# A two-layer diffusion-transformer step on one core: modulation by row sums, w_in's upper parts by casting loads, staged parameters

## The chip, the cores and the metric

The kernel runs on one core of one Trainium2 chip. The metric is the device time of one execution in microseconds. The core has five engines that run their own instruction queues in order: TensorE (PE, with its weight loads as PEld), VectorE (DVE), ScalarE (ACT), GpSimd (POOL) and SyncE (SP). Transfers between HBM and the on-chip memory are issued from the queues of SP, ACT or POOL.

## The reference

Two layers run over 256 latent tokens and 128 context tokens of width 1024, in float32. Each layer computes a modulation, a mixer of 16 heads and a SwiGLU feed-forward part:

```
m   = silu(c) @ w_mod + b_mod              (c: one vector for the latent tokens, one for the context; 6 x 1024 columns)
h   = rms(x) * g_mix * (1 + m[1]) + m[0]
z   = h @ w_in                             (1024 x 2336: q/kv latents, neighbourhood q,k,v, differential q,k,v)
x  += m[2] * (concat(o_mla, o_na, o_df) @ w_out)
h   = rms(x) * g_ffn * (1 + m[4]) + m[3]
x  += m[5] * ((silu(h @ w_gate) * (h @ w_up)) @ w_down)        (inner width 2816)
```

The three mixers are multi-head latent attention (6 heads), two-dimensional neighbourhood attention with learned biases (6 heads) and differential attention (4 heads). The new keys and values of the context are outputs too.

## The kernel before, in words

Tokens lie on the free axis of x (128 partitions x 8 x 384). A product with a weight is made of three float32r matmuls (`mm3`, lines 317 to 320): the weight and the activations are split into an upper part, rounded to float32r, and the rest. For weights, `split_hi` (line 251) copies the raw float32 block to `wh` on ACT, and `split_lo` (line 257) subtracts it on DVE into `wl`. There are three buffers each of raw, `wh` and `wl`; a `wh` buffer is free again when PE has read it for the last time.

**Modulation.** `ModSet` (lines 334 to 403) makes 2048 columns of m: for each of 8 row blocks of 128, one 1 MB load on SP's queue into a raw buffer and four matmuls that have the two vectors as 32 stationary columns (line 369), in four column groups of the array side by side. The set is then copied out on ACT (line 375), turned by four transposes (line 380) and added to b_mod on DVE (line 386). The first 2048 columns of layer 0 are made in four parts before its first norm. The other sets are spread over the stages as follows: layer 0's attention has both remaining sets of layer 0 and the first of layer 1 (24 blocks); the turn from layer 0 to layer 1 has 6 blocks of layer 1's second set, four of which lie in `early` buffers that POOL's queue loads (lines 1549 to 1553); layer 1's attention has the last 2 of these and the third set (10 blocks).

**Attention.** The order of all instructions of a layer's attention is written out by a planner (`Plan.order`, lines 112 to 176): a list scheduler with a duration for each task, one queue per engine, counted buffers (`ROOM`) and priorities. Each engine then gets its tasks in the planned order. `g1` (line 750) multiplies by w_in in 6 column chunks of 4 row blocks each; its tasks and the modulation blocks have low priorities, so the planner puts them between the steps of the softmax chains. `weights` (line 725) plans the load of a block, the upper part on ACT and the lower part on DVE. POOL makes the inverse roots of the norms in this stage (`rsqrt`, lines 509 and 510), which queries and keys wait for, and two-operand steps of the differential heads.

**Feed-forward part.** It is not planned by hand: the framework's scheduler orders the instructions by priority and estimated time. `w_get` makes the parts of a weight block two blocks ahead. A gate/up step m (22 of them) has 48 matmuls, a down step (8 of them) has 66. The buffers `hh` and `hl`, which hold the mixer's input and later its outputs, are free in this stage; `fh` and `fl` hold the input of the gate/up loop.

**Parameters.** `parameters(l)` (line 530) fetches a row of per-column gains to all partitions (`prow`, line 534) and makes rotary tables from it on DVE. For layer 1 the fetch is issued from POOL's queue and is placed as soon as layer 0 has read `prow` for the last time.

## Time and profile before

| what | value |
|---|---|
| median of 3 runs | 1043.28 us (1042.18 to 1043.92) |
| the profiled execution's own time | 1044.4 us |
| its span | 1042.2 us |
| mean granted TensorE clock | 0.995 |
| PE / DVE / ACT / POOL busy | 98% / 61% / 49% / 14% of the span |
| moved by DMA | 160.14 MB, of it 4.69 MB by POOL's queue |

The profile is of one execution. Busy times leave out register, branch, semaphore and DMA-issuing instructions. In the lists of groups a row gives the line, the engine, the operation, what it writes and reads with the shapes, the count, then the busy time in us and the mean of one in ns, then the idle time before them and what ended it. A float32 matmul leaves two records, so a modulation block of four shows as x8.

### The profile page before, as it was taken

Reading aid. Unit: us, or ns where it says so; the run is one execution under the profiler, and the core shown is the slowest. Engines: PE = TensorE matmul, PEld = TensorE weight load, DVE = VectorE, ACT = ScalarE, POOL = GpSimd, SP = SyncE. Lnnn points to the kernel's source line nnn. Section 1 sums busy time; section 2 is a strip of 40 time slices with the busy share of each in tenths; the row PEclk is TensorE's granted clock in tenths of the full one; section 3 lists DMA queues with packets and bytes.
Section 4 is the critical chain, followed back from the end, with each engine's and each line's share of the span. In section 5 each row is a group of like instructions: output and inputs, shape, how many; then the busy total and the mean of one; then the engine's idle time right before and its main releaser. Section 6 shows DMA issues by size and latency. Waiting matters only on the chain.

```text
span 1042.2 us, 16578 instructions
## 1 busy us (share of the span) xinstructions
PE 1025.5 (98%) x6212; PEld 931.2 (89%) x6212; DVE 630.9 (61%) x1447; ACT 509.0 (49%) x1179; POOL 149.9 (14%) x221
## 2 busy tenths in 40 slices
PE   8999999999999999999999999999999999999998
PEld 7877777669999999999978977777999999999998
DVE  4677786767555555544446887777756555554332
ACT  3376777745433443333326567786644333343221
POOL 2266223200000000000016543240000000000000
PEclk9999999999999999999999999999999999999999
DMA  9865548745625343364444245552334344333541
GB/s 360 317 206 185 165 152 298 256 136 161 203 82 161 93 151 111 96 207 123 128 159 155 73 150 169 189 185 81 122 109 135 110 133 122 120 111 111 148 133 45
DMA packets 125999, 160.14 MB, mean 154 GB/s; under 512 B 4704, under 2 KB 111328, under 8 KB 120800
## 3 DMA queue, kind: packets, MB, share of 16 engines
q1 hardware_dynamic: 123552, 153.73, 45.9%
q0 software_dynamic: 784, 4.69, 1.2%
q8 instruction: 49, 0.80, 0.3%
q10 hardware_dynamic: 1584, 0.66, 0.2%
q14 instruction: 30, 0.25, 0.1%
HBM read 156.02 MB, written 3.05 MB: 153 GB/s over the span
## 4 chain that ended last, share of the span: by engine, by line
PE 88%; POOL 4%; DVE 4%; ACT 2%; issue 1%; DMA 1%; ACTq 0%; DVEq 0%; POOLq 0%
PE z L318 13%; PE z L320 12%; PE z L319 12%; PE t L319 6%; PE t L318 6%; PE t L320 6%; PE s L319 6%; PE s L318 6%; PE s L320 6%; PE m L369 4%; PE s L996 3%; POOL small L510 3%; PE t L963 2%; PE t L1098 2%; PE t L1335 1%
## 5 line engine op out<-in xcount | busy, mean ns | idle before, releaser
L251 ACT ACTIVATE wh<-raw 128x1024 fp32r<-128x1024 f32 (+2 forms) x216 | 201.6, 935 | 356.0 <-PE z L319 128.9
L257 DVE TENSOR_TENSOR wl<-raw,wh 128x1024 fp32r<-128x1024 f32 (+2 forms) x216 | 231.2, 1072 | 122.8 <-ACT wh L251 122.6
L318 PE MATMUL z<-fh,wh 128*128 128x386 f32 x304 | 103.2, 339 | 0.0
L319 PE MATMUL z<-fl,wh 128*128 128x386 f32 x304 | 103.0, 339 | 0.0
L320 PE MATMUL z<-fh,wl 128*128 128x386 f32 x304 | 102.6, 338 | 0.0
L318 PE MATMUL z<-wh,hh 128*128 128x384 f32 (+1 forms) x264 | 100.5, 381 | 0.9 <-ACT tok L1203 0.4
L320 PE MATMUL z<-wh,hl 128*128 128x384 f32 (+1 forms) x264 | 90.4, 342 | 0.5 <-DVE hl L490 0.3
L319 PE MATMUL z<-wl,hh 128*128 128x384 f32 (+1 forms) x264 | 89.7, 340 | 0.0
L510 POOL TENSOR_TENSOR small<-small,mhalf 128x4 f32<-128x4 f32 (+4 forms) x58 | 72.2, 1245 | 4.8
L318 PE MATMUL s<-fh,wh 128*128 128x386 f32 x200 | 68.2, 341 | 0.0
L318 PE MATMUL t<-fh,wh 128*128 128x386 f32 x200 | 68.1, 340 | 0.0
L319 PE MATMUL s<-fl,wh 128*128 128x386 f32 x200 | 67.8, 339 | 0.0
L319 PE MATMUL t<-fl,wh 128*128 128x386 f32 x200 | 67.7, 339 | 0.0
L320 PE MATMUL t<-fh,wl 128*128 128x386 f32 x200 | 67.5, 338 | 0.0
L320 PE MATMUL s<-fh,wl 128*128 128x386 f32 x200 | 67.5, 338 | 0.0
L1015 ACT ACTIVATE e<-s,small 128x384 f32<-128x384 f32 (+1 forms) x108 | 54.3, 509 | 16.3 <-DVE small L1004 15.2
L318 PEld LDWEIGHTS z<-wh,hh 128*128 128x128 f32 x264 | 49.8, 189 | 13.1 <-issue 8.2
L319 PEld LDWEIGHTS z<-fl,wh 128*128 128x128 f32 x304 | 57.5, 189 | 0.0
L320 PEld LDWEIGHTS z<-fh,wl 128*128 128x128 f32 x304 | 57.3, 188 | 0.0
L318 PEld LDWEIGHTS z<-fh,wh 128*128 128x128 f32 x304 | 57.2, 188 | 0.0
L996 PE MATMUL s<-ku,qu 96*128 96x384 f32 (+5 forms) x170 | 52.0, 411 | 0.6 <-ACT e L1015 0.6
L319 PE MATMUL z<-ul,wh 128*128 128x384 f32 x154 | 52.4, 340 | 0.0
(305 smaller groups left out, 2321.1 us busy)
## 6 DMA issues: line engine op xcount, KB each, us to landing
raw<-in_w_mod SPq DMA_DIRECT2D x36, 1024.0 KB, 5.1
raw<-in_w_gate SPq DMA_DIRECT2D x22, 1024.0 KB, 5.4
raw<-in_w_up SPq DMA_DIRECT2D x22, 1024.0 KB, 5.4
raw<-in_w_down SPq DMA_DIRECT2D x32, 704.0 KB, 4.5
raw<-in_w_in SPq DMA_DIRECT2D x40, 384.0 KB, 4.0
raw<-in_w_out SPq DMA_DIRECT2D x8, 1024.0 KB, 5.9
qu<-in_w_mod SPq DMA_DIRECT2D x8, 512.0 KB, 6.7
ku<-in_w_mod SPq DMA_DIRECT2D x8, 512.0 KB, 7.4
```

The source lines that it names most:

```text
L251: nc.scalar.activation(hi, src, AF.Copy)
L257: nc.vector.tensor_tensor(lo, src, hi.bitcast(F32), op=ALU.subtract)
L318: nc.tensor.matmul(out, sh, mh, start=first, stop=False)
L319: nc.tensor.matmul(out, sh, ml, start=False, stop=False)
L320: nc.tensor.matmul(out, sl, mh, start=False, stop=last)
L369: nc.tensor.matmul(self.pm[32 * g:32 * g + 32, :n], sv[:, kb + k, :], ws, start=(kb + k == 0), stop=(kb + k == KD - 1), tile_position=(0, ...
L510: nc.gpsimd.tensor_tensor(out, t[:, :n], mhalf[:, :n], op=ALU.pow)
L963: nc.tensor.transpose(pt[:, b, :], x, ident)
L996: nc.tensor.matmul(ps[:, i, :], q, k, start=True, stop=True)
L1015: nc.scalar.activation(x["e"][i], ps[:, j, :], AF.Exp, bias=x["mx"][:, i:i + 1], accum_out=x["su"][:, i:i + 1])
L1098: nc.tensor.matmul(po[64 * i:64 * i + 64, 0:NL], vv[:, b, v0 + i, :], p["pT"][i][:, b, :], start=(b == 0), stop=(b == 2), tile_position=(0 ...
L1335: nc.tensor.matmul(po, x["p"][:, b, :], vd[0][:, b if t < 2 else 3, h, :], start=(b == 0), stop=(b == nb - 1))
```

## The change

**Modulation.** 40 of the 96 column blocks of 128 are no longer made by matmuls: columns 5120 to 6143 of both layers, and columns 0 to 2047 and 4096 to 5119 of layer 1. A new class `RowSums` makes them on DVE in the feed-forward stages. It loads 128 rows of the transposed w_mod (0.5 MB, POOL's queue, three buffers in the room of `hl`), multiplies them by silu(c), which lies in the room of `hh` on all partitions, and adds up along the row with one `tensor_tensor_reduce` for each of the two vectors, starting from b_mod. Layer 0's stage makes one block after each of the gate/up steps 2 to 21 and then 2, 3, 3 and 4 after the first four down steps; layer 1's stage makes one after each of the gate/up steps 2 to 9. The remaining sets are columns 2048 to 4095 of each layer (8 blocks) and columns 4096 to 5119 of layer 0 (4 blocks, each two row blocks of 1024 columns). The `early` loads follow the last row sum, in the room of `fh`, `fl`, `hh` and `hl`.

**w_in.** From chunk 2 on in layer 0 and from chunk 1 on in layer 1 (16 and 20 blocks) the upper part is not copied by ACT: a load from HBM on POOL's queue writes float32r into the `wh` buffer. The raw block is loaded as before, and DVE subtracts as before. The planner has a POOL task of 0.55 for the issue, in the line of the blocks, that takes the `wh` buffer, and a transfer task after it.

**Parameters.** Layer 1's row is loaded into the room of `fl0` and copied to `prow` by ACT.

The host adds the transposed w_mod and the two vectors in rows to the inputs. `RowSums.load` issues as many loads as there are buffers; each further one waits until DVE has read the buffer.

```diff
@@ -38,7 +38,11 @@
 PARAM = (28, 11)
 LAG = 2.8
 SPREAD = ((15, 3), (60, 9))
-DOWN = (0, 0, 0, 0, 0, 0, 0, 0)
+ROWSUMS = ((0, (40, 48)), (1, (0, 16)), (1, (32, 40))), ((1, (40, 48)),)
+ROWS_UP = (0, 0) + (1,) * 20
+ROWS_DOWN = (2, 3, 3, 4, 0, 0, 0, 0)
 PPRIO = (1.0, 2.0, 3.0, 4.0)
 WPRIO = (1.5, 2.5, 3.5, 4.5)
@@ -52,7 +56,8 @@
 PDN, PDD, PDU, PRT1, PRX, PRN, PRM, PRS = (-1.0, -2.0, -6.0, 0.6, 0.0, 0.0, 0.0, 1.0)
 NORMP = -1100.0
 HOPS = {('pe', 'act'): 0.2, ('pe', 'dve'): 0.16, ('act', 'pe'): 0.22, ('dve', 'pe'): 0.27, ('pool', 'dve'): 0.06, ('act', 'dve'): 0.15, ('dve', 'act'): 0.15}
-EXTRA = (8, 135, 7)
+CAST = (2, 1)
 ROOM = {'z': 3, 's': 2, 't': 2, 'raw': 3, 'graw': 2, 'w': 3, 'tok': 4, 'brief': 2, 'row': 5, 'un': 3, 'e': 4, 'pT': 3, 'pd': 2, 'bias': 2}
 CHUNKS = (((0, 416),),) + tuple(tuple((c + 128 * p, 128) for c in (1568, 1824, 2080)) for p in range(2)) + tuple(
...
@@ -334,30 +339,30 @@
     class ModSet:
-        def __init__(self, l, q, pre=(), part=None):
-            self.l, self.q, self.pre, self.w = l, q, pre, {}
+        def __init__(self, l, n, runs, part=None, pre=()):
+            self.l, self.n, self.part, self.pre, self.w = l, n, part, pre, {}
+            self.runs, self.per = runs, 4 // len(runs)
+            self.cols = [c + n * i for c in runs for i in range(self.per)]
+            self.step = 512 // n
             self.kb = 0
-            if part is None:
-                self.n, self.cols = 512, [2048 * q + 512 * g for g in range(4)]
+        def load(self, kb, *kind):
+            if kb < len(self.pre):
+                self.w[kb] = [self.pre[kb].rearrange("p (k c) -> p k c", k=1)]
+                return
+            nr, width = len(self.runs), self.n * self.per
+            if kind and kind[0] == "un":
+                t = [v.rearrange("p h t -> p (h t)")[:, :1024].rearrange("p (k c) -> p k c", k=self.step) for v in self.room()]
             else:
-                n = self.n = 512 // PARTS
-                self.cols = [2 * n * part, 2 * n * part + n, 1024 + 2 * n * part, 1024 + 2 * n * part + n]
-            self.part, self.step = part, 512 // self.n
-        def load(self, kb, *kind):
-            if self.part is not None and kind[0] != "raw":
-                t = [v.rearrange("p h t -> p (h t)")[:, :1024] for v in self.room()]
-            elif self.part is not None:
-                t = raw.tile([P, 2, 1024], F32, tag="raw", name=nm("raw"))
-                t = [t[:, i] for i in range(2)]
-            if self.part is not None:
-                for i in range(2):
-                    nc.sync.dma_start(t[i], w_mod0[self.part, kb // self.step, :, i])
-                self.w[kb] = [v.rearrange("p (k c) -> p k c", k=self.step) for v in t]
-            elif kb < len(self.pre):
-                self.w[kb] = self.pre[kb]
-            elif self.part is None:
-                self.w[kb] = load(mod_rows(self.l, kb, self.cols[0]), [2048])
+                t = raw.tile([P, nr, self.step, width], F32, tag="raw", name=nm("raw"))
+                t = [t[:, i] for i in range(nr)]
+            for i, c in enumerate(self.runs):
+                src = w_mod[self.l, kb * P:(kb + self.step) * P, c:c + width].rearrange("(k p) c -> p k c", p=P)
+                if self.part is not None:
+                    src = w_mod0[self.part, kb // self.step, :, i].rearrange("p (k c) -> p k c", k=self.step)
+                nc.sync.dma_start(t[i], src)
+            self.w[kb] = t
         def mm(self, kb):
@@ -365,8 +370,8 @@
                 for g in range(4):
-                    ws = w[:, g * n:(g + 1) * n] if self.part is None else w[g // 2][:, k, (g % 2) * n:(g % 2) * n + n]
-                    nc.tensor.matmul(self.pm[32 * g:32 * g + 32, :n], sv[:, kb + k, :], ws,
+                    i = g % self.per
+                    nc.tensor.matmul(self.pm[32 * g:32 * g + 32, :n], sv[:, kb + k, :], w[g // self.per][:, k, i * n:(i + 1) * n],
                                      start=(kb + k == 0), stop=(kb + k == KD - 1), tile_position=(0, 32 * g))
@@ -388,11 +393,11 @@
                 mod_aff(self.l, 0, KD // PARTS * self.part, KD // PARTS * (self.part + 1))
-            elif self.q != 1:
-                mod_aff(self.l, self.q // 2, 0, KD)
+            elif self.cols[0] == 4 * DM:
+                mod_aff(self.l, 1, 0, KD)
         def steps(self):
-            for kb in range(self.kb, KD):
+            for kb in range(self.kb, KD, self.step):
                 self.load(kb)
@@ -416,6 +421,35 @@
             pcol[l][:, g0 + k0:g0 + k1].unsqueeze(2).to_broadcast([P, k1 - k0, 2]), op0=ALU.add, op1=ALU.mult)
+    class RowSums:
+        def __init__(self, parts):
+            self.todo = [(l, c) for l, (a, b) in parts for c in range(a, b)]
+            room = act.tile([P, 3 * DM], F32, tag="hh", name=nm("sums"))
+            self.s, self.junk = room[:, :2 * DM].rearrange("p (v k) -> p v k", v=2), room[:, 2 * DM:]
+            self.w = act.tile([P, 3, DM], F32, tag="hl", name=nm("wt"))
+            self.n = self.loaded = 0
+            nc.gpsimd.dma_start(self.s, crow_d.unsqueeze(0).to_broadcast([P, 2, DM]))
+            self.load()
+            nc.scalar.activation(self.s, self.s, AF.Silu)
+        def load(self):
+            while self.loaded < min(self.n + 3, len(self.todo)):
+                l, c = self.todo[self.loaded]
+                nc.gpsimd.dma_start(self.w[:, self.loaded % 3], w_modT[l, c * P:(c + 1) * P])
+                self.loaded += 1
+        def step(self, n):
+            for l, c in self.todo[self.n:self.n + n]:
+                for v in range(2):
+                    nc.vector.tensor_tensor_reduce(self.junk, self.w[:, self.n % 3], self.s[:, v], 1.0,
+                                                   pcol[l][:, PC_BMOD + c:PC_BMOD + c + 1], ALU.mult, ALU.add, mods[l][:, c, v:v + 1])
+                self.n += 1
+                self.load()
+                if l and c in (15, 39):
+                    mod_aff(l, c // 32, 0, KD)
     STREAMS = ((0, NL, 0), (NL, NT, 1))
@@ -527,11 +561,20 @@
         nc.vector.tensor_tensor(out, out, tmp, op=ALU.add)
-    def parameters(l):
+    def parameters(l, staged=None):
         pc = pcol[l]
         prow = par.tile([P, PR_W], F32, tag="prow", name=nm("prow"))
-        fetch = lambda: (nc.sync if l == 0 else nc.gpsimd).dma_start(prow, prow_d[l:l + 1, :].to_broadcast([P, PR_W]))
+        def fetch():
+            rows = prow_d[l:l + 1, :].to_broadcast([P, PR_W])
+            if staged is None:
+                nc.sync.dma_start(prow, rows)
+            else:
+                t = staged.tile([P, PR_W], F32, tag=f"fl{l - 1}", name=nm("staged"))
+                nc.gpsimd.dma_start(t, rows)
+                nc.scalar.activation(prow, t, AF.Copy)
         naq, lam, nlam, subg = (par.tile([P, 1], F32, tag=t, name=nm(t)) for t in ("naq", "lam", "nlam", "subg"))
@@ -576,7 +619,7 @@
             early = []
-            mod_sets = {key: ModSet(*key, pre=early if key == (1, 1) else ()) for key in ((0, 1), (0, 2), (1, 0), (1, 1), (1, 2))}
+            mod_sets = [[ModSet(0, 512, [2 * DM]), ModSet(0, 256, [4 * DM])], [ModSet(1, 512, [2 * DM], pre=early)]]
         es = ExitStack()
@@ -697,7 +740,7 @@
             for part in range(PARTS):
-                ms = ModSet(0, 0, part=part)
+                ms = ModSet(0, 512 // PARTS, [1024 // PARTS * part, DM + 1024 // PARTS * part], part=part)
                 ms.room = lambda: units(3, P)
@@ -722,6 +765,14 @@
             hready[k] = add(DVE, 0.47, lambda k=k, x=x: norm_lo(k, x["t"], hh, hl), after=[b], frees=[a], prio=NORMP + k)
+        def cast_hi(kb, ci):
+            shape = (2, WIDTH[ci])
+            hi = w_part("wh", shape)
+            c0 = 2 * sum(WIDTH[:ci])
+            nc.gpsimd.dma_start(hi, w_in[l, kb // 2, :, c0:c0 + 2 * WIDTH[ci]].rearrange("p (k c) -> p k c", k=2))
+            return hi
         def weights(key, lead=None, prio=-1000.0, pairs=None):
@@ -740,8 +791,17 @@
             n = shape[0] * shape[1]
+            landed = getattr(lead, "mate", lead) if cs.start == 0 and ks.start else lead
+            if key[0] == "in" and key[2] >= CAST[l]:
+                room = w_line["hi"] = add(POOL, 0.55, lambda: w.update(h=cast_hi(key[3], key[2])), after=[w_line.get("hi")], take=("w",), prio=prio)
+                hi = add(DMA, 2.95 / 2048 * n, lambda: None, after=[room], prio=5.0 + len(plan.tasks))
+                lo = add(DVE, 0.1 + 1.05e-3 * n, lambda: w.update(l=split_lo(raws[rk][:, ks, cs], w["h"], shape)),
+                         after=[hi, landed], frees=[lead] if lead else [], prio=prio)
+                w_next[0] += 1
+                return room, lo, w, lead
             hi = add(ACT, 0.1 + 0.85e-3 * n, lambda: w.update(h=split_hi(raws[rk][:, ks, cs], shape)),
-                     after=[getattr(lead, "mate", lead) if cs.start == 0 and ks.start else lead], take=("w",), prio=prio)
+                     after=[landed], take=("w",), prio=prio)
+            w_line["hi"] = hi
             lo = add(DVE, 0.1 + 1.05e-3 * n, lambda: w.update(l=split_lo(raws[rk][:, ks, cs], w["h"], shape)),
...
@@ -1434,10 +1494,8 @@
                 h.need += 1
-        blocks = [(ms, kb, SPREAD[l][0] + SPREAD[l][1] * kb) for ms in (mod_sets[l, 1], mod_sets[l, 2]) for kb in range(ms.kb, KD)]
-        blocks = [(ms, kb, SPREAD[l][0] + SPREAD[l][1] * i) for i, (ms, kb, _) in enumerate(blocks)]
-        if l + 1 < DEPTH:
-            blocks += [(mod_sets[l + 1, 0], kb, EXTRA[1] + EXTRA[2] * kb) for kb in range(EXTRA[0])]
+        blocks = [(ms, kb) for ms in mod_sets[l] for kb in range(ms.kb, KD, ms.step)]
+        blocks = [(ms, kb, SPREAD[l][0] + SPREAD[l][1] * i) for i, (ms, kb) in enumerate(blocks)]
         prev, fin = None, first_mod
@@ -1447,7 +1505,7 @@
             prev = add(PE, 0.93, lambda ms=ms, kb=kb: ms.mm(kb), after=[ld, prev, fin], frees=[ld] if ld else [], prio=DENSE / 2)
-            if kb == KD - 1:
+            if kb + ms.step == KD:
                 a = fin = add(ACT, 0.48, ms.evac, after=[prev], prio=0.0)
@@ -1486,7 +1544,7 @@
         if l + 1 < DEPTH:
-            mod_q.extend(mod_sets[l + 1, q].steps() for q in range(2) if mod_sets[l + 1, q].kb < KD)
+            mod_q.extend(ms.steps() for ms in mod_sets[l + 1])
         for key, w in ahead:
@@ -1516,6 +1574,7 @@
         waiting = []
+        sums = RowSums(ROWSUMS[l])
         for m in range(KF):
@@ -1546,12 +1605,9 @@
             waiting = []
+            sums.step(ROWS_UP[m])
         if l + 1 < DEPTH:
-            for i in range(4):
-                pool, tag = (act, "hh") if i == 0 else (act, "hl") if i == 1 else (ff, f"fh{l}") if i == 2 else (ff, f"fl{l}")
-                early.append(pool.tile([P, 2048], F32, tag=tag, name=nm("early")))
-                nc.gpsimd.dma_start(early[i], mod_rows(l + 1, i, 2048))
-            made_params = parameters(l + 1)
+            made_params = parameters(l + 1, ff)
             made_params[-2]()
@@ -1568,8 +1624,11 @@
                 norm_add(nst, m)
-                if m < 7:
-                    mod_steps(DOWN[m])
+                sums.step(ROWS_DOWN[m])
+                if sums.n == len(sums.todo) and not early:
+                    for i, (pool, tag) in enumerate(((ff, f"fh{l}"), (ff, f"fl{l}"), (act, "hh"), (act, "hl"))):
+                        early.append(pool.tile([P, 2048], F32, tag=tag, name=nm("early")))
+                        nc.gpsimd.dma_start(early[i], mod_rows(l + 1, i, 2048))
             else:
...
@@ -1653,22 +1712,24 @@
+        "crow": np.stack([a["c"][0], a["c_ctx"]]),
+    feeds["w_mod"], feeds["w_modT"] = a["w_mod"], a["w_mod"].transpose(0, 2, 1)
```

More of the change, by code (lines that the diff above doesn't have):

```diff
@@ L179, in trunk @@
 @with_exitstack
-def trunk(ctx: ExitStack, tc, xT_d, cv_d, pcol_d, prow_d, cache_d, dfk_d, rope_d, bias_d, ident_d,
-          w_mod, w_mod0, w_in, w_uq, w_ukv, w_out, w_gate, w_up, w_down, yT_d, new_d):
+def trunk(ctx: ExitStack, tc, xT_d, cv_d, crow_d, pcol_d, prow_d, cache_d, dfk_d, rope_d, bias_d, ident_d,
+          w_mod, w_mod0, w_modT, w_in, w_uq, w_ukv, w_out, w_gate, w_up, w_down, yT_d, new_d):
     nc = tc.nc
@@ L774, in g1 @@
                         done(t, lambda t=t: z[t], u, room[t])
-        g1_state, g1_lead = {}, {}
+        g1_state, g1_lead, w_line = {}, {}, {}
         mlu = []
@@ L1664 @@
     feeds["w_in"] = np.concatenate([np.concatenate([w[..., c:c + n] for c, n in x], axis=4).reshape(L, KD // 2, P, -1) for x in CHUNKS], axis=3)
-    for n in ("w_mod", "w_uq", "w_ukv", "w_out", "w_gate", "w_up", "w_down"):
+    for n in ("w_uq", "w_ukv", "w_out", "w_gate", "w_up", "w_down"):
         feeds[n] = a[n]
@@ L1670 @@
     arrays, args = {}, []
-    order = ("xT", "cv", "pcol", "prow", "cache", "dfk", "rope", "bias", "ident", "w_mod", "w_mod0", "w_in", "w_uq", "w_ukv", "w_out", "w_gate", "w_up", "w_down")
+    order = ("xT", "cv", "crow", "pcol", "prow", "cache", "dfk", "rope", "bias", "ident", "w_mod", "w_mod0", "w_modT", "w_in", "w_uq", "w_ukv", "w_out", "w_gate", "w_up", "w_down")
     for n, v in ((n, feeds[n]) for n in order):
```

## The prediction

> **What bounds the kernel now.** First the page: span, busy times, and the shares of the chain that ended last.
>
> ```profile
> span 1042.2 us, 16578 instructions
> PE 1025.5 (98%) x6212; PEld 931.2 (89%) x6212; DVE 630.9 (61%) x1447; ACT 509.0 (49%) x1179; POOL 149.9 (14%) x221
> ...
> PE 88%; POOL 4%; DVE 4%; ACT 2%; issue 1%; DMA 1%; ACTq 0%; DVEq 0%; POOLq 0%
> ```
>
> TensorE (PE) is busy for 98% of the span and makes 88% of the chain. An average says little about one stage, so next the busy time of each engine by stretch (layer 0's attention, a piece of its gate/up loop and of its down loop, layer 1's projections, layer 1's attention); the columns are PE, weight loads, DVE, ACT, POOL, granted clock, DMA share, GB/s.
>
> ```profile
> 52.00:106.00 54.00, 52.58 (x294) 38.96 (x292) 41.25 (x118) 36.87 (x112) 34.18 (x43) 1.00 0.58 192
> 106.00:229.00 123.00, 120.77 (x790) 86.60 (x790) 89.35 (x258) 84.20 (x272) 27.27 (x48) 0.99 0.64 212
> 280.00:400.00 120.00, 120.00 (x683) 120.00 (x682) 69.89 (x130) 48.37 (x75) 0.00 (x0) 1.00 0.40 124
> 458.00:526.00 68.00, 68.00 (x389) 68.00 (x388) 26.92 (x40) 21.61 (x29) 0.00 (x0) 1.00 0.44 122
> 537.00:614.00 77.00, 72.48 (x411) 60.71 (x410) 56.15 (x142) 44.80 (x123) 43.03 (x59) 1.00 0.38 126
> 614.00:728.00 114.00, 112.51 (x714) 85.44 (x715) 88.69 (x245) 85.97 (x276) 29.54 (x48) 0.99 0.48 159
> ```
>
> PE leaves 2.2 of 123 us idle in the one attention stretch and 1.5 of 114 in the other, and nothing in the feed-forward stretches. The same windows for line 369 alone (the modulation matmuls; 8 records make one 1 MB block) show what the change takes from it:
>
> ```profile
> 52.00:106.00 54.00, 6.39 (x48) 0.94 (x48) 1.00 0.58 192
> 106.00:229.00 123.00, 20.05 (x144) 2.88 (x144) 0.99 0.64 212
> 614.00:728.00 114.00, 10.65 (x80) 1.57 (x80) 0.99 0.48 159
> ```
>
> That is 6 + 18 + 10 = 34 blocks. The chain in order of time (start, length, what) has most of them on it, and has PE alone from 106 to 197; such pieces are
>
> ```profile
> 26.11 1.01 PE m L369 x32
> ...
> 119.00 0.44 PE t L380 x4
> ...
> 617.37 0.99 PE m L369 x8
> ```
>
> So a block costs 0.99 us, four narrow steps (x32) 1.01, and one turned set 0.44. From 584 to 616 the chain is another one, the roots of the norms on POOL; its shares there and a piece of it:
>
> ```profile
> by line: POOL small L510 32.7%; POOL small L509 11.0%; DVE dfo L1231 8.7%; issue 7.5%; DVE wl L257 5.9%; DVE small L1242 4.8%; DVE tok L1245 4.6%; DVE rt L1226 4.4%; ACT wh L251 2.6%; DVE tok L893 2.4%; PE t L1294 2.0%; PE z L318 1.8%; PE z
> ...
> 600.46 2.16 POOL small L510
> ```
>
> **The change part by part.** The sum is made on the profiled execution's own 1044.4 us (span 1042.2 and 2.2 around it), 1.1 above the median 1043.28.
>
> *Fewer modulation blocks on PE.* Layer 0's attention keeps 8 wide blocks and 4 blocks of two narrow steps instead of 24; layer 1's keeps 2 instead of 10. Twenty blocks go: 20 x 0.99 = 19.8. Of the transposes at line 380 two whole sets and half a third go, 2.5 x 0.44 = 1.1. PE loses 20.9 us where it is the bound. Evacuation and bias of those sets lie beside PE and count nothing.
>
> *The stall at the end of layer 0's attention.* The timeline (start, length, instruction, idle before it and its releaser):
>
> ```profile
> 209.18 0.65 POOL L534 DMA_DIRECT2D prow<-in_prow  x1 [0.30 <-POOL brief L1162]
> ...
> 215.21 0.18 DVE L545 TENSOR_SCALAR prow<-prow 128x32 f32<-128x32 f32 x1 [1.03 <-DMA prow<-in_prow]
> ...
> 217.88 0.52 PE L963 MATMUL t<-ident,e 128*128 128x128 f32 x3 [2.11 <-DVE small L1020]
> ...
> 220.29 1.94 PE L369 MATMUL m<-raw,sv 128*32 128x512 f32 x8
> ```
>
> DVE waits 1.03 us for layer 1's parameter row in the middle of layer 0's last softmax, then works on its tables before the maximum PE needs; PE idles 2.11 and runs its next block at about half speed, 1.94 for 0.99. With the row staged in the fl0 buffer, which is in use until the gate/up loop ends, neither the load nor the tables can come here. Gain 0 (another chain ends as late) to 2.11 + 0.95 + 1.0 = 4.1; I take 2.5, since the idle is certain and the slow block only follows it. The load then sits in POOL's queue behind the row-sum loads, and an ACT copy waits for it in the down loop; there DVE and ACT have 41 and 46 of 68 us free.
>
> *Casting loads.* 16 blocks in layer 0 and 20 in layer 1 lose their ACT copy and get a second read of HBM (36 x 0.39 = 14 MB), issued by POOL. Prices:
>
> ```profile
> L251 ACT ACTIVATE wh<-raw 128x768 fp32r<-128x768 f32 x72 | 60.8, 845 | 76.2 <-PE z L319 22.6 <-PE s L319 15.1 <-PE t L319 15.0
> L257 DVE TENSOR_TENSOR wl<-raw,wh 128x768 fp32r<-128x768 f32 x72 | 69.4, 965 | 33.4 <-ACT wh L251 33.3
> ...
> raw<-in_w_in SPq DMA_DIRECT2D x40, 384.0 KB, 4.0
> early<-in_w_mod POOLq DMA_DIRECT2D x4, 1024.0 KB, 6.2
> ...
> 444.37 1.12 POOL L1553 DMA_DIRECT2D early<-in_w_mod  x2 [176.67 <-PE s L320]
> ```
>
> ACT is freed of 36 x 0.845 = 30 us, which is beside PE and counts nothing by itself. POOL takes 36 issues of 1.12/2 = 0.56 us. No row shows a load that casts; between the 4.0 us of the same size from SP's queue and the 6.2 of 1 MB from POOL's I take 4.5. The issue stands in POOL's in-order queue and waits until PE has freed one of three wh buffers; behind it wait the roots, and behind those PE's transposes. Inside the POOL-bound stretches lie layer 1's chunks 1 and 2 (8 loads) and layer 0's chunk 2 (4): 12 x 0.56 = 6.7 if all lie on the chain, 0 if none; I take 3, about half, since POOL is busy 43 of 77 us there. A freed buffer is full again after 0.56 + 4.5 + 0.97 = 6.0 us, where copy and subtraction took 0.85 + 0.97 = 1.8. PE needs 18 matmuls for a block, 18 x 120/683 = 3.2, so the two other buffers cover 6.3: just enough. Bounds 0 and, with 6.2 to land and 0.6 late for each of layer 1's first ten, 6; I take 1.5.
>
> *Row sums on DVE.* 32 blocks of 128 columns in layer 0's feed-forward stage, 8 in layer 1's, each one 0.5 MB load and two passes over 128x1024 with an accumulator. No row shows that operation. Nearest:
>
> ```profile
> L257 DVE TENSOR_TENSOR wl<-raw,wh 128x1024 fp32r<-128x1024 f32 x104 | 126.9, 1222 | 27.7 <-ACT wh L251 27.7
> L1004 DVE TENSOR_REDUCE small<-s 128x1 f32<-128x384 f32 x72 | 38.1, 553 | 5.5 <-PE s L996 4.6
> L1015 ACT ACTIVATION_READ_ACCUMULATOR e<-s,small 128x1 f32 x108 | 22.0, 204 | 0.0
> L1545 DVE SCALAR_TENSOR_TENSOR gt<-gt,small,gt 128x256 f32<-128x256 f32 x44 | 21.3, 484 | 4.1
> L1545 DVE SCALAR_TENSOR_TENSOR gt<-gt,small,gt 128x128 f32<-128x128 f32 x44 | 15.2, 346 | 0.0
> ```
>
> Lower bound: one pass and a read-out, 1.22 + 0.20 = 1.43, a block 2.9. Upper bound: product and reduction one after the other, 1.22 + 0.55 x 1024/384 = 2.70, a block 5.4. A gate/up step is 48 matmuls, so 683/48 = 14.2 steps in 120 us: 8.43 us each, of which DVE works 69.89/14.2 = 4.91. One block fits at 2.9 (7.8 of 8.43), not at 5.4. A down step of 66 matmuls takes 11.5 us with 4.6 on DVE; three blocks at 2.9 overrun it by 1.8 and four by 4.7, which the four steps without blocks take up. I take the lower price (it is the nearest row in form: two fp32 inputs, same width) and 1 us for both layers together, for the silu on 128x2048 behind a broadcast load early in the stage, where ACT is 40% busy. Bounds 0 and 44 (rival 2).
>
> The row above for line 1545 goes (484 - 346)/128 = 1.08 ns per element with two fp32 inputs. [...]
>
> *Queues and bytes.* The 20 MB of modulation weights that leave SP's queue are read by POOL's in the feed-forward stages, where it issues nothing but four early loads and a root. Those early loads move behind the last row sum; the sums end about a step after the fourth of eight down steps, which leaves three steps, 35 us, for loads of 6.2. In the attention stretches the DMA share is 0.64 and 0.48, and layer 0 reads 12 MB less and 6 more. I count 0; were the early loads late, PE would wait at the turn of the layers for what is missing of 6.2.
>
> *Less cover.* With 20.9 us less to run, PE meets more of the waits of the softmax chains. After the change DVE would work some 88 of 108 us in layer 0's main stretch, 81% for 73%. In 537:614, where no such blocks fill in, PE idles 4.5 of 77, 6%; the attention stretches idle 3.7 of 237 now. At 6% of 216 they would idle 13, 9 more. Bounds 9 and, if ACT's relief removes the waits there are, -3.7; I take 4.5, half the loss, since the measured stretches have the same mix of work.
>
> Sum: -20.9 - 2.5 + 3 + 1.5 + 1 + 4.5 = **-13.4**, 1031.0 on the profiled execution's scale, 1029.9 on the median's. Own range of this forecast: 1023 to 1037.
>
> **The rivals.**
>
> 1. *The plan packs as tightly as before.* All 20.9 and 4.1 come, and the casts hide: 1043.3 - 25 = 1018. For it: the chain is PE alone for 90 us of layer 0. Against: DVE at 81%.
>
> 2. *DVE becomes the bound of gate/up* because a row-sum pass needs more than (8.43 - 4.91)/2 = 1.76 us. At 2.70 each step overruns by 1.9: 20 + 8 steps give 52, the down loop 12 x 5.4 + 8 x 4.6 - 92 = 9 more; two weight blocks ahead hide 8.4 in each layer: +44. Then 1043.3 - 14.4 + 44 = 1073, slower. Against: the slope of line 1545.
>
> 3. *POOL's queue blocks.* Each cast waits for PE to free a wh buffer, with roots behind it. The copy's idle row shows 76.2 us before 72 copies, 1.06 each, now ACT's; put on POOL's chain for 36 loads that is 38 us, and with the issue 36 x 1.62 = 58. If a third reaches the end: 1043.3 - 17.9 + 19 = 1044; if half, 1054. It turns slower where more than 0.5 us per cast comes through (17.9/36). [...]
>
> 4. *The blocks were mere filler:* softmax latency holds the attention's length and only the stall goes, 1040. Against: PE's unbroken chain.
>
> **How the numbers follow.** Forecast 0.49, rival 1 0.20, rival 2 0.06, rival 3 0.12, rival 4 0.13. Forecast, rival 1 and most of rival 4 (0.11) are faster by over 0.2% (2 us, about what a measurement here can tell): 0.80. Rival 3 splits 0.04 same, 0.08 slower; with the rest of rival 4, same is 0.06, and with rival 2 slower is 0.14. The range goes from 1015, a little beyond rival 1, to 1044, which takes in rival 4 and the mild case of rival 3.
>
> **What would show it.** Line 369 should have 14 blocks in the attention stretches instead of 34. The DVE wait on the parameter load at the end of layer 0's attention should be gone. The row sum's mean should be near 1.3 to 1.5 us, with PE still unbroken in gate/up. POOL's issue should stay near 0.6, and no idle of PE over 1 us should lead back to a cast. Wrong would be: a longer stretch between layer 1's norm and its first scores by more than 5 us, PE idle in gate/up, or attention stretches that shrink by less than half of 20.9.

## The result, and the profile after

The changed kernel takes 1036.34 us (median of six executions, 1033.49 to 1040.18), the kernel before 1043.24 beside it: a ratio of 0.9943 between the means, 95% interval 0.9919 to 0.9967. It is faster, as forecast, but by 6.9 us between the medians (6.0 between the means) where 13.4 were forecast. The profiled execution took 1035.82 us by its own time, 8.6 less than the one of before.

The page of the changed kernel: span, busy times, shares of the chain that ended last, the row sums, and the DMA rows of the row sums' and the casting loads.

```profile
span 1034.0 us, 16556 instructions
PE 1013.9 (98%) x6074; PEld 932.5 (90%) x6074; DVE 718.6 (69%) x1599; ACT 480.7 (46%) x1144; POOL 197.0 (19%) x299
...
PE 84%; POOL 6%; DVE 5%; ACT 2%; DMA 2%; issue 1%; ACTq 0%; DVEq 0%; POOLq 0%
...
L446 DVE CUSTOM_DVE_ANT_0 sums<-wt,sums,pcol 128x1024 f32<-128x1024 f32 x80 | 102.2, 1278 | 0.0
...
wt<-in_w_modT POOLq DMA_DIRECT2D x40, 512.0 KB, 4.3
...
wh<-in_w_in POOLq DMA_DIRECT2D x36, 384.0 KB, 3.8
```

The issues of the casting loads and the row sums one by one (shortest, median and longest in ns, first and last start):

```profile
L773 POOL DMA_DIRECT2D wh<-in_w_in x36: 527/616/653, 50.6 to 665.6; - x36
...
L446 DVE DVE_READ_ACCUMULATOR2_ANT mod<- x80: 76/82/86, 261.1 to 813.8; 128x1 f32 x80
```

A row-sum pass takes 1.28 us, and each is followed by a read-out of 0.08. TensorE has 11.6 us less busy time, not 20.9: part of what is left takes longer.

Busy time by stretch (PE, weight loads, DVE, ACT, POOL, granted clock, DMA share, GB/s), and below it line 374 alone, the modulation matmuls:

```profile
106.00:219.00 113.00, 110.16 (x721) 86.60 (x722) 85.69 (x239) 77.95 (x263) 34.40 (x54) 0.97 0.48 151
280.00:400.00 120.00, 120.00 (x682) 120.00 (x681) 113.47 (x206) 45.21 (x71) 10.04 (x19) 1.00 0.63 207
```

```profile
52.00:106.00 54.00, 6.39 (x48) 0.94 (x48) 1.00 0.72 237
106.00:219.00 113.00, 6.41 (x80) 1.98 (x80) 0.97 0.48 151
606.00:620.00 14.00, 2.13 (x16) 0.32 (x16) 1.00 0.68 220
```

In gate/up DVE is now busy for 113 of 120 us and PE still has no gap. Line 374 has the 14 blocks that were to stay: 6 wide ones, 2 wide and 4 of two narrow steps, 2 in layer 1. After 160 us in layer 0 and after 617 in layer 1 there are none.

Stage by stage, from the first matmul that reads `fh` (gate/up), `uh` (down) and `dg` (the norm's spread at the start of layer 1):

| stretch | before | after | difference |
|---|---|---|---|
| start to layer 0's gate/up | 255.8 | 245.5 | -10.3 |
| layer 0's gate/up | 188.3 | 188.2 | -0.1 |
| down and turn of the layers | 97.2 | 98.5 | +1.3 |
| layer 1's attention (spread to gate/up) | 216.2 | 216.8 | +0.6 |
| layer 1's gate/up, down and end | 284.7 | 285.0 | +0.3 |

Layer 1's attention lost 8 blocks of 0.99 us and gained nothing. Where they went is seen in three rows of each kernel: the last matmul of the projections, the last product with the softmax weights, and the window between them, called the tail. Before, then after:

```profile
L319 PE MATMUL z<-wl,hh x144: 331/337/358, 545.3 to 694.8; 128*128 128x384 f32 x120, 128*128 128x416 f32 x24
...
L1098 PE MATMUL t<-pT,vn x36: 379/379/431, 701.8 to 729.9; 128*64 128x256 f32 x36
...
694.80:729.90 35.10, 33.76 (x207) 23.68 (x207) 26.12 (x81) 23.82 (x76) 6.17 (x10) 0.95 0.29 100
```

```profile
L324 PE MATMUL z<-wl,hh x144: 331/338/358, 536.2 to 678.3; 128*128 128x384 f32 x120, 128*128 128x416 f32 x24
...
L1158 PE MATMUL t<-pT,vn x36: 379/379/687, 689.7 to 721.5; 128*64 128x256 f32 x36
...
678.30:721.50 43.20, 40.51 (x206) 28.11 (x207) 30.09 (x89) 27.20 (x90) 6.95 (x11) 0.80 0.13 39
```

The projections end 153.5 us after the spread (541.3) before and 146.1 after it (532.2) now: 7.4 earlier, the price of the blocks. The tail then takes 43.2 us instead of 35.1, with 206 matmul records instead of 207 (16 of the 207 are two modulation blocks, none of the 206; with the projections over earlier, more of the softmaxes lie in the tail). Its granted clock is 0.80 instead of 0.95; at full clock, by an estimate from these numbers, the two would be alike, 43.2 x 0.80 = 34.6 and 35.1 x 0.95 = 33.3. The tail in steps of 4 us:

```profile
692.00:696.00 4.00, 2.65 (x18) 1.93 (x16) 3.86 (x11) 3.49 (x11) 0.00 (x0) 1.00 0.09 32
696.00:700.00 4.00, 3.66 (x12) 1.80 (x10) 3.65 (x12) 1.43 (x7) 0.00 (x0) 0.64 0.00 0
700.00:704.00 4.00, 3.68 (x12) 2.49 (x12) 1.86 (x7) 3.04 (x12) 0.00 (x0) 0.50 0.19 53
704.00:708.00 4.00, 4.00 (x12) 2.48 (x13) 2.49 (x9) 1.62 (x5) 1.12 (x2) 0.50 0.01 2
708.00:712.00 4.00, 4.00 (x15) 2.02 (x15) 2.84 (x9) 1.68 (x5) 0.00 (x0) 0.50 0.00 0
712.00:716.00 4.00, 4.00 (x28) 2.81 (x25) 1.53 (x6) 2.42 (x7) 0.00 (x0) 0.73 0.01 2
```

PE is busy for 2.65 of 4 us while DVE has 3.86; then the clock falls to half for some 17 us, and in that time PE shows as almost fully busy (3.66 to 4.00 of 4 us from 696 to 712) with about half as many records (12 to 15 in each window, 27 to 30 from 716 on). An average of PE's busy share (98%) hides this. Layer 0's tail has the same:

```profile
188.00:192.00 4.00, 4.00 (x12) 2.29 (x10) 3.46 (x13) 2.64 (x11) 1.61 (x3) 0.56 0.07 18
192.00:196.00 4.00, 4.00 (x23) 2.49 (x22) 3.86 (x11) 2.00 (x6) 0.00 (x0) 0.58 0.12 26
```

"Clock lost" in what follows is the sum of 4 us x (1 - granted clock) over the 4-us windows of an attention part (from 150 us on in layer 0, from the spread on in layer 1): 3.4 and 8.6 us after, 1.7 and 1.7 before. The six executions of the changed kernel line up by it: mean clock 0.992 goes with 1033.5 us, 0.987 with 1035.8 to 1036.5, 0.984 and 0.985 with 1040.2.

All runs in one table. Times are medians; the ratios are taken over all executions, each against those of the kernel before that ran beside it, so they are not quotients of the medians. The stretches and clocks are of each profiled execution, whose own time can lie a few microseconds off the median. Layer 0 is from the start to gate/up, layer 1 from the spread to gate/up.

| kernel | us | ratio to before | layer 0 | layer 1 | clock lost in each |
|---|---|---|---|---|---|
| before | 1043.2 | 1 | 255.8 | 216.2 | 1.7, 1.7 |
| after | 1036.3 | 0.994 [0.992, 0.997] | 245.5 | 216.8 | 3.4, 8.6 |
| e1 no casts | 1037.3 | 0.995 [0.994, 0.997] | 244.6 | 217.4 | 1.7, 10.2 |
| e2 casts in layer 0 | 1035.9 | 0.994 [0.992, 0.996] | 242.0 | 218.0 | 0, 10.7 |
| e3 late blocks, layer 1 | 1027.6 | 0.986 [0.983, 0.988] | 247.8 | 209.3 | 3.4, 2.4 |
| e4 constant matmuls | 1033.1 | 0.991 [0.990, 0.993] | 246.6 | 211.6 | 0, 0.8 |
| e5 late blocks, both | 1019.3 | 0.978 [0.976, 0.980] | 238.2 | 205.7 | 0, 0 |
| e6 e4 without casts | 1028.1 | 0.986 [0.984, 0.988] | 240.5 | 214.7 | 0, 3.4 |
| e7 e4 without staging | 1037.1 | 0.995 [0.993, 0.997] | 253.8 | 210.8 | 3.7, 0 |
| e8 before, early blocks | 1042.3 | 1.000 [0.999, 1.002] | 254.5 | 214.6 | 1.7, 3.4 |
| e9 e5 without casts | 1049.4 | 1.006 [1.005, 1.007] | 252.1 | 223.8 | 6.8, 15.4 |
| e10 e5, casts in layer 1 | 1035.0 | 0.993 [0.991, 0.995] | 256.1 | 208.6 | 12.0, 1.7 |
| e11 e5 without staging | 1031.1 | 0.989 [0.988, 0.990] | 253.1 | 205.8 | 10.2, 0 |
| e12 after, order kept, constant matmuls | 1031.5 | 0.990 [0.988, 0.991] | 242.2 | 214.3 | 0, 1.7 |
| e13 row sums alone | 1043.0 | 1.000 [0.999, 1.001] | 254.0 | 217.3 | 8.5, 10.2 |
| e14 after without staging | 1034.6 | 0.993 [0.991, 0.994] | 244.8 | 221.1 | 3.4, 10.3 |
| e15 casts alone | 1044.4 | 1.003 [1.000, 1.005] | 254.0 | 215.4 | 1.7, 0 |
| e16 other late blocks | 1026.3 | 0.983 [0.982, 0.984] | 238.5 | 213.7 | 0, 4.4 |

### The profile page after: what moved, and what is told of

The parts are those of the page before. It is cut to its first block, busy times and chain, and to the rows that moved or that the text cites. A ratio compares the mean times of both kernels' runs of the same rounds, so it can differ in the third digit from the quotient of the medians.

```text
span 1034.0 us, 16556 instructions
## 1 busy us (share of the span) xinstructions
PE 1013.9 (98%) x6074; PEld 932.5 (90%) x6074; DVE 718.6 (69%) x1599; ACT 480.7 (46%) x1144; POOL 197.0 (19%) x299
## 4 chain that ended last, share of the span: by engine, by line
PE 84%; POOL 6%; DVE 5%; ACT 2%; DMA 2%; issue 1%; ACTq 0%; DVEq 0%; POOLq 0%
PE z L323 12%; PE z L324 11%; PE z L325 11%; PE t L324 6%; PE t L323 6%; PE t L325 6%; PE s L324 6%; PE s L323 6%; PE s L325 6%; PE s L1056 3%; POOL small L544 3%; PE t L1023 2%; PE m L374 2%; PE t L1158 2%; DMA wh<-in_w_in 1%
## 5 line engine op out<-in xcount | busy, mean ns | idle before, releaser
L256 ACT ACTIVATE wh<-raw 128x1024 fp32r<-128x1024 f32 (+3 forms) x180 | 171.3, 953 | 358.4 <-PE z L324 134.9
L446 DVE CUSTOM_DVE_ANT_0 sums<-wt,sums,pcol 128x1024 f32<-128x1024 f32 x80 | 102.2, 1278 | 0.0
L440 POOL DMA_DIRECT2D wt<-in_w_modT x40 | 21.5, 537 | 271.4 <-DVE mod L446 190.8
L1075 ACT ACTIVATE e<-s,small 128x384 f32<-128x384 f32 (+1 forms) x101 | 51.4, 516 | 16.3 <-DVE small L1064 14.7
```

The source lines that it names most:

```text
L256: nc.scalar.activation(hi, src, AF.Copy)
L440: nc.gpsimd.dma_start(self.w[:, self.loaded % 3], w_modT[l, c * P:(c + 1) * P])
L446: nc.vector.tensor_tensor_reduce(self.junk, self.w[:, self.n % 3], self.s[:, v], 1.0, pcol[l][:, PC_BMOD + c:PC_BMOD + c + 1], ALU.mult, A ...
L1075: nc.scalar.activation(x["e"][i], ps[:, j, :], AF.Exp, bias=x["mx"][:, i:i + 1], accum_out=x["su"][:, i:i + 1])
```

## The experiments

### Are the casts to blame? e1 and e2

```diff
-CAST = (2, 1)
+CAST = (6, 6)   # e1: none; e2: (2, 6), layer 0 alone
```

> The changed kernel with all upper parts of w_in copied by ScalarE again; the row sums and the staged parameters stay. Clock theory (with so few modulation blocks left in the attention tails TensorE has nothing to fill its gaps with, its granted clock is halved there, and that eats the removed work): the tails stay as thin, the mean granted clock stays near 0.987 (before 0.995), and the time stays within 2 us of the changed kernel's 1036.3. Cast theory (the loads on GpSimd's queue and their latency lengthen layer 1's projections by 4.8 us: 79.2 us from the norm's spread to the first local scores, against 74.4 before): those 74.4 us come back and the time is 1030 to 1033. Latency theory (the softmax chains on VectorE and ScalarE set the attention, whatever TensorE has to do): with 36 copies of about 0.8 us back on ScalarE the attention gets longer, 1037 to 1042.

> The changed kernel with the casting loads in layer 0 alone; layer 1 copies on ScalarE as before. Cast theory: layer 1's projections go back from 79.2 to about 74.4 us and the time is about 1031.5. Clock theory: layer 1's first scores may come earlier, but its tail near 700 us stays at half clock, so layer 1's attention still ends 224 to 226 us after the norm's spread, and the time is 1034.5 to 1037.5. Latency theory: ScalarE has 20 copies more in layer 1, 1037 to 1040.

1037.3 and 1035.9 us: the same as the change within the intervals, with layer 1's tail as slow (10.2 and 10.7 us of clock lost). The cast theory falls. The first time also lies in the latency theory's range, the second only in the clock theory's. The cast theory's premise was a misreading besides: the group taken for the first scores was a later one. The first stands 58.1 us after the spread in the changed kernel against 66.5 before, 8.4 earlier, and at 66.7 and 67.1 without casts in layer 1. So in these orders of work the scores come earlier with the casts, and the tail gives it back.

### Filler put into the tails: e3, e5, e16

```diff
-SPREAD = ((15, 3), (60, 9))
+SPREAD = ((15, 3), (132, 6))   # e3: the two blocks of layer 1 come due late
 # e5: layer 0's last four at 146, 152, 158, 164 too; e16: 148 to 166, and 128, 136
```

> The changed kernel with layer 1's last two modulation blocks due at 132 and 138 us of its plan instead of 60 and 69, so that they fall into its attention tail (the planner's order changes with them). Clock theory: the granted clock in 20-us windows of 680 to 720 us rises from 0.93 and 0.65 to above 0.85, and layer 1's attention is 2 to 5 us shorter: 1031.5 to 1034.5. Latency theory: two blocks of 1 us each move, the tail keeps its length, 1036 to 1038. Cast theory: nothing in the projections changes but 2 us of filler are gone from them, 1035.5 to 1038.

> The changed kernel with layer 1's last two modulation blocks due at 132 and 138 us of its plan, as in the run of the late blocks (1027.6 there), and layer 0's last four due at 146 to 164 us instead of 39 to 48. Clock theory: layer 0's tail keeps its clock too (0.56 and 0.58 in 188 to 196 us of the changed kernel), its attention ends at 240 to 243 us instead of 245.5 to 248, the runs lie closer together, and the time is 1021 to 1026. Latency theory: layer 0's end stays at 245 to 248 us whatever fills its gaps, 1027 to 1030.

> The run with both layers' late blocks (1019.3) with layer 0's last four blocks due 2 us later (148 to 166) and layer 1's two at 128 and 136 instead of 132 and 138. Clock theory: any placement that leaves filler in the tails holds the clock, 1018 to 1024, with both tails at a granted clock of 0.97 or more. If the first placement was a lucky order, 1026 to 1034.

Two blocks moved, then six, no work added or removed: 1036.3, then 1027.6, then 1019.3 us, both better than the clock theory's ranges. Layer 1's tail in e5:

```profile
669.00:703.70 34.70, 33.32 (x218) 23.50 (x219) 27.49 (x86) 25.05 (x83) 6.96 (x11) 1.00 0.33 107
```

34.7 us at full clock. Against the profiled execution of the changed kernel layer 0 is 7.3 us shorter and layer 1 11.1. If each microsecond of lost clock counts in full, the clock accounts for 12.0 of these 18.4 us; the rest fits six blocks at 0.99 us that no longer stand in a stretch where PE has no gap, but that was not measured by itself. e16 missed the clock theory's range and lies at the near end of the one for a lucky order: 1026.3. It holds the clock in layer 0 (238.5) and in layer 1's tail (1.00 from 670.1 to 706.9 us), and loses 4.4 us elsewhere in layer 1, of it 3.4 at 713 to 726, around two waits of PE for weights of w_out (1.8 and 1.5 us). So these three late placements beat the change clearly, and which one is chosen still decides 7 us. All three keep the change's casts and staging; with the casts taken out, late blocks did not hold the clock (e9 and e10 below).

### Useless matmuls: e4 and e12

In e4 the planner gives them out as its last choice, and finds another order. In e12 the order of the changed kernel stays as it is:

```diff
+            end = 0.0
             for t in work:
+                if t.eng == PE and t.dur:
+                    if FILL[l][0] <= t.start <= FILL[l][1]:
+                        for _ in range(min(int((t.start - end) / 0.25), 3)):
+                            warm()        # one 128x128 matmul of ones, read by nobody
+                    end = t.start + t.dur
                 t.fn(...
```

> The changed kernel with 128x128 matmuls of the constant tile ones added to TensorE's order in the two attention tails, up to 32 in layer 0 and 36 in layer 1, each given out only where the plan has nothing else for TensorE; no result of theirs is read. Clock theory: the granted clock in the tails goes from 0.5 to 0.7 up to 0.95 to 1.0, layer 0's attention ends about 2 us earlier and layer 1's 5 to 8 us earlier, 1027 to 1031. Latency theory: the clock goes up but the chains on VectorE and ScalarE set the pace, and each added matmul can hold up a needed one by some 0.25 us: 1035 to 1040. Cast theory: no change of the projections, 1035 to 1038.

> The changed kernel with its order of work as it is, every instruction on every engine in the same place, and 27 matmuls of the constant tile ones put into TensorE's order where the plan has a gap of 0.25 us or more in the attention tails (12 in layer 0, 15 in layer 1); no result of theirs is read. Clock theory: the granted clock of layer 1's tail goes from 0.80 to above 0.9, the tail from the last projection matmul to the last turned weight (43.2 us in the changed kernel, 35.1 before) takes 36 to 40 us, and the time is 1028 to 1033. Order theory (what helped in the runs with late blocks and constant matmuls was the new order that the planner found, not the clock): the tail keeps its 43 us, 1036 to 1039.

```profile
680.30:717.20 36.90, 36.19 (x239) 27.70 (x239) 30.04 (x89) 26.76 (x90) 6.96 (x11) 1.00 0.16 48
...
L1546 PE MATMUL m<-ones x54: 270/275/377, 171.7 to 704.7; 128*128 128x128 f32 x54
```

With 27 matmuls (54 records) added and nothing else changed, layer 1's tail goes from 43.2 us at clock 0.80 to 36.9 at 1.00, and the time from 1036.3 to 1031.5. In layer 0, 3.4 us less clock lost come out as 3.3 us. The order theory falls; this is the cleanest run for the clock. Of the 6.3 us that layer 1's tail gives back, only 2.5 show in the table, because in this execution the projections before it take 149.9 us instead of 146.1:

```profile
606.40:610.40 4.00, 2.15 (x9) 2.15 (x10) 3.83 (x17) 0.49 (x1) 1.91 (x2) 0.79 0.60 197
610.40:614.40 4.00, 4.00 (x18) 3.69 (x18) 3.74 (x11) 1.62 (x5) 0.62 (x1) 0.78 0.56 155
```

There PE waits 2.0 us on DVE and 1.7 us of clock are lost, long before layer 1's first added matmul (687.9); the changed kernel's profile has neither. e4 has 51 such matmuls and 1033.1, between the ranges of the clock and the latency theory: of 11.2 us less clock lost only 3.6 come through (1035.8 to 1032.2 in the profiled executions). The added matmuls take PE time too, and the order is another; how much is due to which was not measured.

### The reverse on the kernel before: e8

```diff
-SPREAD = ((15, 3), (60, 9))
+SPREAD = ((15, 3), (10, 2))   # in the kernel before
```

> The kernel before, with its same work, but layer 1's modulation blocks due from 10 us on, 2 us apart, instead of from 60 us, 9 us apart, so that none is left for its attention tail. Clock theory: the tail falls to a granted clock of 0.5 to 0.7 for some 15 to 20 us as in the changed kernel, layer 1's attention (216.2 us from the norm's spread to the first gate matmul) gets 3 to 8 us longer, and the time is 1045 to 1051. Latency theory: the same work in another order, 1041 to 1044.

```profile
L369 PE MATMUL m<-raw,sv x96: 592/593/618, 541.7 to 650.1; 128*32 128x512 f32 x96
...
691.90:727.00 35.10, 33.99 (x187) 23.29 (x187) 25.90 (x78) 23.41 (x76) 7.52 (x11) 0.90 0.15 45
```

A miss for the clock theory: 1042.3 lies in the latency theory's range. No block starts after 650.1 us, and the tail keeps its 35.1 us, though with 187 records instead of 207; it loses 3.4 us of clock instead of 1.7, not 8 to 10, and layer 1's attention gets 1.6 us shorter. So a tail without filler need not fall for long. The planner's order probably decides, by how it spaces the softmaxes; why this order has its clock back after some 7 us at half, and the changed kernel's only after 17, stays open.

### The parts alone: e13, e14, e15

e13 is the change with `CAST = (6, 6)` and the parameter row loaded straight into `prow`; e14 has only the latter; e15 is the kernel before with the casting loads.

```diff
             if staged is None:
-                nc.sync.dma_start(prow, rows)
+                (nc.sync if l == 0 else nc.gpsimd).dma_start(prow, rows)
...
-            made_params = parameters(l + 1, ff)
+            made_params = parameters(l + 1)
```

> The row sums alone: the changed kernel without casting loads and with layer 1's parameter row loaded straight into its tile. By the prediction's terms (20.9 for the blocks, 1 for VectorE, the softmax's lost cover) it is 16 to 18 us faster than before, 1024 to 1027. Clock theory: the stall on the parameter row at the end of layer 0's attention comes back and falls into a tail with no filler, as in the late-block run without staging; layer 0's attention ends at 246 to 256 us, and the time is 1036 to 1044.

> The changed kernel with the parameter row loaded straight into its tile: what the staging is worth in the change itself. The prediction's term is 2.5 us (0 to 4.1): 1036.5 to 1040.5. Clock theory: VectorE stands 2 us at the load and has 13 small instructions behind it in the middle of the tail's softmaxes; TensorE falls to half clock for 10 to 20 us, layer 0's attention ends at 250 to 257 us instead of 245.5, and the time is 1041 to 1048.

> The kernel before with the casting loads alone, from the same chunks on as in the change. The prediction's terms for them are 3 us of GpSimd's issue time and 1.5 of landing latency: 1046 to 1049. If they are neutral, as in the runs without them (1037.3 and 1035.9 against 1036.3), 1041.5 to 1043.5. If ScalarE's freed time is worth something while filler is still there, 1036 to 1041.

The row sums alone, which take the work of 20.9 us off PE, are worth nothing: 1.0003 [0.9994, 1.0011]. The profiled execution loses 18.7 us of clock, 15.3 more than the kernel before. With the staging they are worth 0.46% (e1), with the casts 0.72% (e14), with both 0.57%. The casts alone cost 0.25% [0.01, 0.49], between the ranges of "neutral" and of the prediction's price; most of it comes from two of the twelve executions (1053.8 and 1054.0), and the other ten are 1.0 us above the kernel before in the mean. e14 missed its range on the good side: in its profile the parameter load has landed by the time DVE comes to it, and e14 and the change cannot be told apart. The parts do not add up, and the last column of the table shows much of why: what a part is worth depends on how long PE stays at half clock.

### Staging and casts where the tails have filler: e6, e7, e9, e10, e11

> The run with the constant matmuls in the tails (1033.1) with the casting loads taken out: what the casts are worth where the clock is held. Cast theory: they cost some microseconds, and the time is 1028 to 1031. Latency theory: ScalarE's copies (36 of about 0.8 us) are in the way of the softmax, 1034 to 1039. If neither, the same within 1 us, 1032 to 1034.

> The run with the constant matmuls in the tails (1033.1) with layer 1's parameter row loaded straight into its tile, as in the kernel before: its load then waits in GpSimd's queue for the last reader of layer 0's row. As the prediction had it, 2.5 us come back at the end of layer 0's attention and the turn to its gate and up stage: 1034.5 to 1037. If the stall was hidden or lies elsewhere, 1032.5 to 1034.

> The run with both layers' late blocks (1019.3) with all casting loads taken out, so that ScalarE makes the upper parts again. If the casts cost nothing and give nothing, 1018 to 1021. If, as the prediction had it, they cost 4.5 us of latency and GpSimd's issue time, 1014 to 1017. If ScalarE's 36 copies are in the softmax's way once the clock is held, or the order of work that the plan finds with them is worse, 1022 to 1030.

> The run with both layers' late blocks (1019.3) with the casting loads in layer 1 alone. It says which layer the difference of the run without casts lies in: layer 1's attention stays at 205 to 207 us from the norm's spread to the first gate matmul, and layer 0's end (238.2) moves by what the casts are worth there: to 234 to 236 if they cost, 238 to 239 if they are neutral, 241 to 246 if ScalarE's copies are in the way.

> The run with both layers' late blocks (1019.3) with layer 1's parameter row loaded straight into its tile, waiting in GpSimd's queue for the last reader of layer 0's row. As the prediction had it, 2.5 us (at most 4.1) come back: 1021 to 1023.5. If the wait reaches further (as the 4 us of the run without staging and with the constant matmuls suggest, 1037.1 against 1033.1), 1023 to 1028. If hidden, 1018.5 to 1020.5.

e6 (1028.1) lies in the cast theory's range. e7 (by 0.1 us), e9, e10 and e11 came out slower than any range written down for them. e11 has e5's order, with layer 1's parameter instructions in layer 0's tail, and 1031.1 for 1019.3: the staging is worth 11.8 us there, 4.1 between e4 and e7. The stall and what follows, from the parameter row's view and the windows of e11:

```profile
  DMA prow<-in_prow: 2.3, 1
...
188.00:192.00 4.00, 0.86 (x10) 0.43 (x6) 2.97 (x19) 0.72 (x3) 0.90 (x2) 1.00 0.78 260
192.00:196.00 4.00, 3.62 (x12) 2.24 (x12) 3.83 (x13) 1.90 (x7) 0.52 (x1) 0.52 0.17 47
196.00:200.00 4.00, 4.00 (x22) 1.74 (x22) 2.84 (x8) 1.63 (x6) 0.00 (x0) 0.50 0.02 6
```

DVE stands 2.3 us at the load and then has 1.6 us of tables to make, which hold up the softmax for some 4 us in all; PE waits 3.5 us and is busy for 0.86 of 4; then 20 us pass at half clock (10.2 us lost), and layer 0's attention is 14.9 us longer (253.1 for 238.2), nearly four times the hold-up.

The casts have no price of their own in these runs. Taken out of e4's kernel they leave it 5 us faster (e6), taken out of e5's 30 us slower (e9), with 22.2 us of clock lost, and out of layer 0 alone 16 us slower (e10). The planner orders the whole layer anew each time; these runs price the orders, not the loads.

e9 and e10 also bound the lesson of the late blocks. Their blocks are due as late as e5's, and e9 is still slower than the kernel before. In layer 1's tail of e9 the clock is down from about 695 us, and the first of its two blocks runs only at 701.8:

```profile
694.80:698.80 4.00, 4.00 (x12) 1.76 (x10) 3.35 (x11) 2.16 (x7) 1.21 (x3) 0.59 0.06 16
698.80:702.80 4.00, 4.00 (x17) 1.88 (x16) 2.38 (x6) 2.31 (x7) 0.00 (x0) 0.50 0.00 0
```

In e10's layer 0 the clock falls at 198 us, after the last block (189.6). Before each fall of the clock in the attention parts of these two runs no block had run for 4 us or more. A late due time alone did not hold the clock. In e5, whose layer 1's tail has 1.00, the two blocks run inside the tail, their matmuls starting at 679.0 to 685.5: by these runs the filler has to stand where PE runs thin.

## Why the prediction was right and wrong, point by point

- *Fewer modulation blocks, -20.9.* Right in count and in price where they stood: in layer 1 the projections end 7.4 us earlier for 8 blocks of 0.99. The version that holds the clock (e5) is 23 us faster than before, close to rival 1's 25, though with six blocks elsewhere.
- *The stall, -2.5 (0 to 4.1).* The wait is gone, as forecast. The term was treated as a fixed price and is none: it came out as about 0 (e14 against the change), 5 (e13 against e1), 4 (e7 against e4) and 12 (e11 against e5). The row quoted in the prediction, a block of 1.94 us for 0.99 behind the stall, was the clock at half for 3.4 us (1.7 us lost in the table); I took it for a side effect worth 1 us.
- *Casting loads, +3 and +1.5.* Issue 0.61 us (0.56 forecast), landing 3.8 (4.5). Alone they cost 1.5 us between the medians, in the change nothing measurable: the 4.5 was too dear by about 3 or more. (The upper bound of 6 does not follow from its own terms: 0.56 + 6.2 + 0.97 against 6.3 of cover is 1.4 late, not 0.6; at 3.8 to land it did not come to that.) Rival 3 falls. The issues took 0.53 to 0.65 us, and 34 of the 36 overlapped with a VectorE instruction.
- *Row sums on DVE, +1.* Right. A pass and its read-out take 1.28 + 0.08 = 1.36 us against a threshold of 1.76; gate/up keeps its length, and in down PE has no gap up to 520 us. The 1.3 us of the third stretch lie in the turn of the layers, where PE waits 0.8 on ACT. Rival 2 falls. The pass, CUSTOM_DVE_ANT_0 in the profile, takes 1.28 us for 1024 elements, near the 1.22 of the plain subtraction in the prediction's rows.
- *Queues and bytes, 0.* Right: the early loads are in time; one of the blocks they feed now runs at 445.8 us, in the down loop. The order was not as told: the last row sum of layer 0 ends at 452.6 us, in the second down step, and two of the four early loads are issued before that (434.6 and 439.8).
- *Less cover, +4.5 (-3.7 to 9).* **This step failed.** I priced PE's idle time alone, 6% of the attention, and put the clock at nothing. What came is a state: in layer 1 PE thins out to two thirds busy (2.65 of 4 us), its clock is halved for some 7 us in layer 0 and 17 in layer 1, and matmuls in that time take up to nearly double (the longest t<-pT,vn 687 ns, the median 379). Had the blocks and the stall come in full, the attention would be 23.4 us shorter; it is 9.7, so 13.7 were lost where cover and casts stood at 9.0. Of these 13.7, 8.6 are clock lost more than before (1.7 in layer 0, 6.9 in layer 1), by the windows of one execution each. The other 5.1 are near the 4.5 of the term; which waits make them up was not taken apart. A clock column stood in every window that I quoted, with 0.99 in the attention stretches, and I read it as 1.
- *Rival 4, mere filler, 1040.* Nearest to what happened in layer 1, for another reason: in the tail it is mostly the clock that holds the length, and not the latency of the softmax alone (e12). For the row sums alone its outcome, without the stall's gain, is the measured one.

Of the signs named, the one for "wrong" fired: the attention stretches shrank by 10.3 - 0.6 = 9.7 us, less than half of 20.9.

## What to carry to other kernels

Before taking work off a busy TensorE, look at the stretch where it last has slack, in windows of about 4 us, and at the clock column: filler that seems to cost its full time may be what holds the clock there (in e12, with 27 useless matmuls added in the two tails, the clock of layer 1's went from 0.80 to 1.00). Try to move what filler is left to the thin spot itself, and look at the clock again, since being late is not enough (e9, e10). Take out small stalls of other engines there first: one cost nearly four times its length (e11). When one edit's worth swings with another's, compare the clock lost before comparing times: here six blocks in another place were worth 17 us, more than the change itself, and made the best version measured (e5, 1019.3 us, ratio 0.978).

## What the runs showed of the hardware that was not expected

The clock fell without a long gap. In the changed kernel's layer 1 the longest wait of PE between 676 and 700 us is 1.0 us, by the view of waits:

```profile
PE s L1056 <- ACT e L1075: 1.0, 1, 1.0
```

The clock fell after PE was idle for 1.35 of 4 us (692 to 696) in pieces of at most 1.0. No threshold comes out of the runs: in layer 1's tail of e15 PE is busy for only 3.00 of 4 us (696 to 700) and the clock stays at 1.00, and in the kernel before it falls after 3.19 of 4 (710 to 714).

The time at half clock came in steps. Clock lost is mostly a multiple of 1.7 us (1.7, 3.4, 8.5, 10.2, 12.0, 15.4), so the time at half clock came to a multiple of 3.4 us: one step in either layer of the kernel before, two and five in the change, six in layer 0 of e11. In e16's 4.4 us, 1.0 lies in the first window of the count (525.7 to 529.7, clock 0.75) and the other 3.4 are two steps; e2's 10.7, e3's 2.4, e4's 0.8 and e7's 3.7 are off the steps as well. What makes the steps, no run shows. The tails stayed down for long while the profile shows PE as busy: 17 us here, and 20 in e11, with PE at 3.62 to 4.00 of 4 us.
